# A hybrid RWKV-7 and DeltaNet layer on one core: a block inverse stepped on 32x32 tiles, and a third of the modulation sums moved behind the woven part

## Chip, cores and metric

One Trainium2 chip, one of its cores. The metric is the device time of one execution in microseconds (us); three timed runs of the kernel before gave 2334.98 to 2337.48, median 2336.01.

## What is computed

One layer over 256 latent tokens with 256 context tokens, width 2048, fp32. Cut to what matters here:

```python
mod = silu(c) @ w_ada + b_ada                 # 6 x 2048 columns
sh1, sc1, gt1, sh2, sc2, gt2 = split(mod, 6)
h = rmsnorm(x, norm1_w) * (1 + sc1) + sh1     # the same for the context: hc
# two token mixers on h @ w_in, hc @ w_in, in both directions of time
o_a = rwkv7(...)      # 16 heads of 64, chunked in the kernel: needs (I + L)^-1 of 64 x 64 blocks
o_b = gdn(...)        # 8 heads of 128, chunks of 64: needs (I + L)^-1 too
m = sigmoid(g_a) * (o_a @ p_a) + sigmoid(g_b) * (o_b @ p_b)
x = x + gt1 * (m @ w_out)
x = x + gt2 * swiglu(rmsnorm(x, norm2_w) * (1 + sc2) + sh2)
return rmsnorm(x, final_norm_w)
```

The second scale is `sc2`, columns 4 x 2048 to 5 x 2048 of `mod`. Of the six blocks of 1024 columns that the kernel calls `ada_rest`, blocks 0 and 1 are gt1, 2 and 3 are sh2, 4 and 5 are sc2.

## The kernel before, in words

**Products.** Weights come from HBM as fp32 chunks of up to 8 x 128 rows by 128 columns (`raw`, 512 KB). ScalarE rounds a chunk to fp32r (`hi`, L356), VectorE subtracts to get the rest (`lo`, L357), and `gemm` (L366 to L368) issues three products per 128 rows: hi by Xh, hi by Xl, lo by Xh. Three raw buffers and two each of hi and lo are in flight. Loads go out on SP's queue.

**Stages.** First the modulation of the first norm (to some 130 us). Then the *woven part*, to some 1388 us: generators for the input products (`products`, `cast`), the RWKV pairs (`prepare`, `grams`, `inverse`, `values`, `scan`, eight pairs of heads), the eight DeltaNet heads (`features`, `tokens`, `decays`, `head_grams`, `head_inverse`, `head_scan`) and `ada_rest`. Then merge A (`o_a @ p_a`, L1496), merge B (`o_b @ p_b`, L1514), the output product (L1528), which also casts four tiles of the first FFN weights, and the FFN with its 44 gate and up tiles and 16 down tiles.

**What sets the order.** In the woven part a planner (`Weave`, L169) runs the generators: each yields operations, the planner gives each a duration by formulas (`Lane`; a small matmul costs 0.024 us if its contraction is under 64 rows, L132), takes the operation that can start first, a lower rank winning ties, and emits it. PE, VectorE, ScalarE and POOL then run that order whatever the real times are. The RWKV pairs have ranks from 0, the heads from 100, the sums of `ada_rest` rank 500 and the products 900. Behind the woven part the framework orders instructions by its own timeline, except those kept in program order.

**The inverse** (`invert`, L552). Per call `nu` units of two 64x64 triangular blocks (16 for an RWKV pair, 8 for a DeltaNet head), half for each direction. The 16x16 blocks on the diagonal are inverted by VectorE (15 pairs of multiply and add, L583), after a round trip through DRAM that lays them out; T0 and its transpose Tx then hold them. The step from 16x16 to 32x32 (L613 to L624) runs once per direction: a group of 64x64 matmuls with 32 moving columns, a multiply with the mask `qmask`, a second group, an add into T0, and a transpose into Tx. The step from 32x32 to 64x64 (L641 on) works on 32x32 tiles of the array. `head_inverse(h)` waits for `inv`, h - 1, and builds the 128x128 inverse (TF) at its end; `head_scan(h)` needs it.

**The sums** (`ada_rest`, L1423). Per block and 128 rows of `w_ada`: one load of 128 x 1024 on POOL's queue, and two VectorE operations of 512 columns that multiply by silu(c) and add to `acc` (ScalarE for the first rows). After 16 of them four matmuls with ones sum over the partitions, VectorE copies the row out, two transposes turn it, and it is added to the bias into `mod`. In merge A POOL also multiplies each product with its gate (L1517), and ScalarE's sigmoids (L1500) wait for one load of 4 MB of gates.

Of the kernel before, what the change touches and what calls it, by code (L numbers as in the profile page):

```python
# [35 lines left out]
_C = {}  # L36
_n = 0
for _name, _w in (("ident", 128), ("ones", 128), ("bd64", 128), ("rmask", 256),
                  ("qmask", 64), ("tri", 256), ("aft", 256), ("q4", 4), ("q2", 2),
                  ("eps", 1), ("gneps", 1)):  # L40
    _C[_name] = (_n, _n + _w)
    _n += _w
# [12 lines left out]
def const_array():  # L55
    c = np.zeros((P, NC_COLS), np.float32)

    def put(name, a):
        lo, hi = _C[name]
        c[:, lo:hi] = np.asarray(a, np.float32).reshape(P, hi - lo)  # L60

    i = np.arange(P)
    put("ident", np.eye(P))
    put("ones", np.ones((P, P)))
    put("bd64", (i[:, None] // 64) == (i[None] // 64))
    s, t = (i % 64)[:, None], np.arange(64)[None]
    put("rmask", np.concatenate([t > s, t >= s, t < s, t <= s], 1))
    rb, cb = s // 16, t // 16
    same = (rb // 2) == (cb // 2)
    even = np.arange(64) // 16 % 2 == 0  # L70
    put("qmask", np.concatenate([(same & (rb % 2 == 1))[:, even], (same & (rb % 2 == 0))[:, ~even]], 1))
    u = i[:, None]
    v = i[None]
    put("tri", np.concatenate([u <= v, u >= v], 1))
    put("aft", np.concatenate([u > v, u < v], 1))
    put("q4", (i[:, None] % 4) == np.arange(4)[None])
    put("q2", (i[:, None] % 2) == np.arange(2)[None])
    put("eps", np.full((P, 1), 1e-6))
    put("gneps", np.full((P, 1), 64e-5))
    return c  # L80
# [30 lines left out]
class Lane:  # L111
# [5 lines left out]
    def __getattr__(self, name):  # L117

        def op(out, *a, **k):
# [6 lines left out]
            if name == "transpose" and len(a) == 2:  # L126
                cost = 0.109
            elif split:
                cost = 0.0065 + 0.000443 * n
            elif name == "matmul":  # L130
                rows, m = a[0].shape[0], out.shape[0]
                if rows < 64:  # L132
                    cost = 0.024
                elif rows == 64:
                    cost = max(0.066, 0.027 + 0.0008 * n)
                elif rows < P or m == P:
                    cost = 0.0054 + 0.00167 * n
                else:
                    cost = 0.107
            else:  # L140
                cost = self.fixed + self.each * n
# [126 lines left out]
def emit(ctx: ExitStack, tc, A, out, dbg=None):  # L268
# [31 lines left out]

    ident, ones, bd64 = c_("ident"), c_("ones"), c_("bd64")
    rmask = c_("rmask").rearrange("p (d k) -> p d k", d=2)
    qmask = c_("qmask").rearrange("p (d a c) -> p d a c", d=2, a=2)
    tri = c_("tri").rearrange("p (d t) -> p d t", d=2)
    aft = c_("aft").rearrange("p (d t) -> p d t", d=2)
    eps, gneps = c_("eps"), c_("gneps")
# [245 lines left out]
    def invert(pool, Lt, parts, nu, which, full, fill):  # L552
# [49 lines left out]
            return Tx[64 * h:64 * h + 64, u, :]  # L602


        def half(t, d):
            ax = "p u"[:2 * len(t.shape) - 3]
            return t.rearrange(f"{ax} (a b c) -> {ax} a b c", a=2, b=2)[..., d, :]

        def mm(ps, d, lhs, rhs):
            return [e.matmul(ps[64 * h:64 * h + 64, 32 * i:32 * i + 32], lhs(h, h2 * d + i), rhs(h, h2 * d + i),  # L610
                             start=True, stop=True) for i in range(h2) for h in range(2)]

        Qm = xt[:, :32 * nu].rearrange("p (u c) -> p u c", c=32)  # L613
        for d in range(2):
            T0d = half(T0[:, us[d]], d)
            ps = yield pib
            yield mm(ps, d, Lt, lambda h, u: half(N_(h, u), d))
            pv = ps[:, 0:32 * h2].rearrange("p (i a c) -> p i a c", a=2, c=16)
            yield v.tensor_mul(Qm[:, us[d]].rearrange("p i (a c) -> p i a c", a=2), pv,
                               qmask[:, d].unsqueeze(1).to_broadcast([P, h2, 2, 16]))  # L620
            yield mm(ps, d, Nt_, lambda h, u: Qm[64 * h:64 * h + 64, u, :])
            yield v.tensor_add(T0d, pv, T0d)
            weave.release(pib)
            yield v.transpose(Tx[:, us[d]], T0[:, us[d]])  # L624


        quads = []
# [795 lines left out]
    def ada_rest():  # L1423
# [20 lines left out]
                    yield s.activation(a, w[:, n:n + 512], AF.Identity, scale=ck[:, 0, 0:1])  # L1444
            weave.ready("added", i)

        for i in range(6 * KT):
            if i > 2:
                yield "added", i - 3
            weave.add(500, row_tile(i))  # L1450
# [33 lines left out]


    wstep[0] = 8
    gates_ctx = ExitStack()
    gp = gates_ctx.enter_context(tc.tile_pool(name="gp", bufs=1, reuse_waits="tile", side="right"))
    PA = gp.tile([P, KT, T], F32, name="PA")
# [6 lines left out]
    for j in range(KT):  # L1496
        ps = pst(pmm, "mm")
        gemm(ps[:, 0:T], load_w(A["pa"][j], P, 8), Oa, T)
        S.copy(PA[:, j], ps[:, 0:T])
        tc.keep_in_program_order(S.activation(gts[:, 2 * j:2 * j + 2, :], gts[:, 2 * j:2 * j + 2, :], AF.Sigmoid))  # L1500
    tc.keep_in_program_order(S.preload_act_table_set(LNEXP))

# [11 lines left out]
    for j in range(KT):  # L1514
# [4 lines left out]
        V.tensor_mul(m, ps[:, 0:T], gts[:, 16 + j])  # L1519
        V.tensor_add(m, m, PA[:, j])  # L1520
        split(M[0][:, j], M[1][:, j], m)

    gates_ctx.close()
    zap = ent(tc.tile_pool(name="zap", bufs=1, reuse_waits="tile", side="right"))
# [3 lines left out]
    for j in range(KT):  # L1528
# [3 lines left out]
        sq = square_sum(x1p, x1[:, j, :], ssum, j == 0)  # L1532
        if 0 < j < KT - 1:
            V.tensor_add(ssum, ssum, sq)
        if j % 3 == 2 and j < 12:
            w4.append(load_w(A["wgu"][j // 3], P, KT, into=[W4[:, i, j // 3] for i in range(2)] + [zap]))
    r = rms_scale(x1p, [ssum, sq], T, "rs")
    m_ctx.close()


    with tc.tile_pool(name="fp", bufs=1, reuse_waits="tile") as fp:
# [157 lines left out]
```

## Time and profile before

| what | value |
|---|---|
| median of three timed runs | 2336.01 us |
| the profiled execution, own time | 2348.77 us |
| its span from the first to the last instruction | 2346.7 us |
| busy share of the span: PE, VectorE, ScalarE, POOL | 95%, 66%, 45%, 5% |
| mean granted TensorE clock | 0.975 of full speed |

A row of the trace gives the engine (PE matmuls, DVE VectorE, ACT ScalarE, POOL, SP), the line of the code, the operation, out<-in by names and shapes. In the woven part every instruction has the line of the planner's helper, L142, so tiles tell them apart: `pi` is the inverse's accumulator, `mm` the products', `aw` the sums' tiles. A matmul busy time is not its cost in a stream; the distance between starts is.

### The profile page before, as it was taken

What the parts mean: (1) busy time and instruction counts of PE and PEld (TensorE: products, weight loads), DVE (VectorE), ACT (ScalarE), POOL (GpSimd) and SP (SyncE); (2) the same over time, 40 slices, a digit from 0 to 9 for tenths busy, and PEclk for the clock granted to TensorE, in tenths of its full rate; (3) what the DMA queues carried; (4) which work ended last, traced back from release to release, by engine and by line L of the source; (5) the groups of instructions that cost most, each with busy time, mean ns of one, the idle gap of its engine ahead of it and who ended that gap; (6) DMA issues with size and microseconds to landing.
All of it is one profiled execution on the core that took longest, in us unless ns stands there. A gap on an engine that the chain in (4) does not pass through costs nothing. (4 is left out here: it accounts for less than half of the span.)

```text
span 2346.7 us, 51488 instructions
## 1 busy us (share of the span) xinstructions
PE 2223.8 (95%) x21368; PEld 1951.7 (83%) x21368; DVE 1557.2 (66%) x3237; ACT 1047.9 (45%) x1863; POOL 113.5 (5%) x183
## 2 busy tenths in 40 slices
PE   7988999999999999999798999999999999999998
PEld 4767677778788777776677989999999999999997
DVE  3447588778986489889878645765666556545454
ACT  3246454544355544344234346544444444444443
POOL 0000000000000011111111003000000000000000
PEclk9999999999999999999789999999999999999999
DMA  9956454434344256657466565663777776566665
GB/s 377 397 148 189 152 134 102 111 83 117 100 109 133 85 172 207 189 167 217 145 191 194 182 219 180 209 214 107 239 233 234 234 238 218 187 185 194 191 191 165
DMA packets 232570, 430.58 MB, mean 183 GB/s; under 512 B 114832, under 2 KB 130064, under 8 KB 227984
## 3 DMA queue, kind: packets, MB, share of 16 engines
q1 hardware_dynamic: 204688, 351.78, 48.4%
q0 software_dynamic: 13824, 50.34, 7.0%
q10 hardware_dynamic: 13824, 25.17, 3.5%
q8 instruction: 167, 2.74, 0.5%
q14 instruction: 67, 0.55, 0.1%
HBM read 401.45 MB, written 25.77 MB: 182 GB/s over the span
## 5 line engine op out<-in xcount | busy, mean ns | idle before, releaser
L357 DVE TENSOR_TENSOR wlo<-wraw,whi 128x1024 fp32r<-128x1024 f32 x328 | 393.5, 1200 | 351.1 <-ACT whi L356 348.2
L356 ACT CAST whi<-wraw 128x1024 fp32r<-128x1024 f32 x328 | 337.7, 1030 | 472.8 <-PE mm L367 413.8
L142 PE MATMUL mm<-hxh,wlo 128*128 128x256 f32 (+1 forms) x1376 | 468.3, 340 | 9.9 <-DVE wlo L142 9.7
L142 PE MATMUL mm<-hxh,whi 128*128 128x256 f32 (+1 forms) x1376 | 469.0, 341 | 3.4 <-ACT whi L142 3.3
L142 PE MATMUL mm<-hxl,whi 128*128 128x256 f32 (+1 forms) x1376 | 468.3, 340 | 0.0
L368 PE MATMUL mm<-hfh,wlo 128*128 128x256 f32 x1344 | 377.1, 281 | 0.4 <-DVE wlo L357 0.4
L366 PE MATMUL mm<-hfh,whi 128*128 128x256 f32 x1344 | 376.5, 280 | 0.0
L367 PE MATMUL mm<-hfl,whi 128*128 128x256 f32 x1344 | 375.2, 279 | 0.0
L142 PEld LDWEIGHTS mm<-hxh,wlo 128*128 128x128 f32 x1376 | 265.6, 193 | 39.4 <-DVE wlo L142 13.0
L142 PEld LDWEIGHTS mm<-hxh,whi 128*128 128x128 f32 x1376 | 265.6, 193 | 31.5 <-issue 6.5
L142 PEld LDWEIGHTS mm<-hxl,whi 128*128 128x128 f32 x1376 | 265.8, 193 | 27.2 <-issue 6.1
L142 DVE TENSOR_TENSOR wlo<-wraw,whi 128x512 fp32r<-128x512 f32 x344 | 236.2, 690 | 62.7 <-ACT whi L142 60.0
L142 ACT CAST whi<-wraw 128x512 fp32r<-128x512 f32 x344 | 205.8, 618 | 112.1 <-PE mm L142 88.9
L366 PEld LDWEIGHTS mm<-hfh,whi 128*128 128x128 f32 x1344 | 253.4, 189 | 0.0
L368 PEld LDWEIGHTS mm<-hfh,wlo 128*128 128x128 f32 x1344 | 252.8, 188 | 0.6 <-DVE wlo L357 0.6
L367 PEld LDWEIGHTS mm<-hfl,whi 128*128 128x128 f32 x1344 | 253.2, 188 | 0.0
L142 DVE TENSOR_TENSOR arena<-arena 128x28 f32<-128x28 f32 (+13 forms) x538 | 132.0, 247 | 32.1 <-DMA arena<-scr 20.4
L366 PE MATMUL mm<-za,whi 128*128 128x256 f32 x512 | 141.8, 277 | 0.0
L367 PE MATMUL mm<-za,whi 128*128 128x256 f32 x512 | 141.7, 277 | 0.0
L368 PE MATMUL mm<-za,wlo 128*128 128x256 f32 x512 | 141.6, 277 | 0.0
L142 DVE SCALAR_TENSOR_TENSOR aw<-aw,ck 128x512 f32<-128x512 f32 x180 | 131.2, 739 | 5.1 <-DMA aw<-ada_rest 4.4
L368 PEld LDWEIGHTS mm<-za,wlo 128*128 128x128 f32 x512 | 96.2, 188 | 0.0
(311 smaller groups left out, 3924.5 us busy)
## 6 DMA issues: line engine op xcount, KB each, us to landing
wraw<-w SPq DMA_DIRECT2D x172, 512.0 KB, 4.3
wraw<-wgu SPq DMA_DIRECT2D x168, 512.0 KB, 4.5
aw<-ada_rest POOLq DMA_DIRECT2D x96, 512.0 KB, 4.7
aw<-ada_first SPq DMA_DIRECT2D x32, 1024.0 KB, 11.5
wraw<-wdn SPq DMA_DIRECT2D x64, 448.0 KB, 3.7
wraw<-wout SPq DMA_DIRECT2D x32, 512.0 KB, 4.7
aw<-ada_gt ACTq DMA_DIRECT2D x64, 256.0 KB, 5.0
wraw<-wdn SPq DMA_DIRECT2D x32, 512.0 KB, 3.6
```

The source lines that it names most:

```text
L142: return Op(self, cost, lambda: getattr(self.engine, name)(out, *a, **k), split)
L356: S.copy(hi[:, c, :M], raw[:, c, :M])
L357: V.tensor_sub(lo[:, c, :M], raw[:, c, :M], hi[:, c, :M].bitcast(F32))
L366: E.matmul(ps, hi, Xh[:, k, :n], start=first and i == 0, stop=False)
L367: E.matmul(ps, hi, Xl[:, k, :n], start=False, stop=False)
L368: E.matmul(ps, lo, Xh[:, k, :n], start=False, stop=last and i == len(wt) - 1)
```

## The change

It makes the 16-to-32 step of both directions at once on 32x32 tiles: one group of matmuls of 32 rows by 16 columns into `pv[:, 0]`, two multiply-adds with a row mask `low16` and an identity `eye16`, a second group into `pv[:, 1]`, copies of the new 16 columns into T0 (four by VectorE, four by ScalarE), and one transpose of all of T0. The planner's price of a small matmul changes with it. And `ada_rest` ends after four blocks; the generator `scale2` does blocks 4 and 5 with operations of 1024 columns, one tile per product of merge A, one per product from the 14th of merge B, and the rest in the output product.

```diff
@@ class Lane
                 if rows < 64:
-                    cost = 0.024
+                    cost = 0.009 if n <= 16 else 0.0125
@@ def invert
-        def half(t, d):
-            ax = "p u"[:2 * len(t.shape) - 3]
-            return t.rearrange(f"{ax} (a b c) -> {ax} a b c", a=2, b=2)[..., d, :]
-
-        def mm(ps, d, lhs, rhs):
-            return [e.matmul(ps[64 * h:64 * h + 64, 32 * i:32 * i + 32], lhs(h, h2 * d + i), rhs(h, h2 * d + i),
-                             start=True, stop=True) for i in range(h2) for h in range(2)]
-
-        Qm = xt[:, :32 * nu].rearrange("p (u c) -> p u c", c=32)
+        fours = [(h, u, 32 * b, slice(64 * h + 32 * b, 64 * h + 32 * b + 32)) for u in range(nu) for h in range(2) for b in range(2)]
+        Qm = xt[:, :16 * nu].rearrange("p (u c) -> p u c", c=16)
+        ps = yield pib
+        pv = ps[:, 0:32 * nu].rearrange("p (k u c) -> p k u c", k=2, c=16)
+        yield [e.matmul(pv[r, 0, u], Lt(h, u)[b:b + 32, b:b + 32], T0[r, u, b + 16 * (u // h2):b + 16 * (u // h2) + 16],
+                        start=True, stop=True) for h, u, b, r in fours]
         for d in range(2):
-            T0d = half(T0[:, us[d]], d)
-            ps = yield pib
-            yield mm(ps, d, Lt, lambda h, u: half(N_(h, u), d))
-            pv = ps[:, 0:32 * h2].rearrange("p (i a c) -> p i a c", a=2, c=16)
-            yield v.tensor_mul(Qm[:, us[d]].rearrange("p i (a c) -> p i a c", a=2), pv,
-                               qmask[:, d].unsqueeze(1).to_broadcast([P, h2, 2, 16]))
-            yield mm(ps, d, Nt_, lambda h, u: Qm[64 * h:64 * h + 64, u, :])
-            yield v.tensor_add(T0d, pv, T0d)
-            weave.release(pib)
-            yield v.transpose(Tx[:, us[d]], T0[:, us[d]])
+            yield v.scalar_tensor_tensor(Qm[:, us[d]], pv[:, 0, us[d]], low16[:, d:d + 1],
+                                         eye16[:, d].unsqueeze(1).to_broadcast([P, h2, 16]), ALU.mult, ALU.add)
+        yield [e.matmul(pv[r, 1, u], Tx[r, u, b:b + 32], Qm[r, u, :], start=True, stop=True) for h, u, b, r in fours]
+        for h in range(2):
+            yield [(s.copy if h else v.tensor_copy)(T0[r, us[d], b + 16 * d:b + 16 * d + 16], pv[r, 1, us[d]])
+                   for d in range(2) for b in (0, 32) for r in (slice(64 * h + b, 64 * h + b + 32),)]
+        weave.release(pib)
+        yield v.transpose(Tx, T0)
@@ def ada_rest
-        for i in range(6 * KT):
+        for i in range(4 * KT):
@@ behind the woven part
+    adp = ad_ctx.enter_context(tc.tile_pool(name="adp", bufs=1, reuse_waits="tile"))
+    def scale2():
+        for b in (4, 5):
+            acc = adp.tile([P, 1024], F32, tag="acc", name="acc")
+            for k in range(KT):
+                w = adp.tile([P, 1024], F32, tag="aw", name="aw", bufs=3)
+                G.dma_start(w, A["ada_rest"][b, :, k, :])
+                if k:
+                    tc.keep_in_program_order(V.scalar_tensor_tensor(acc, w, ck[:, k, 0:1], acc, ALU.mult, ALU.add))
+                else:
+                    tc.keep_in_program_order(V.tensor_scalar_mul(acc, w, ck[:, 0, 0:1]))
+                if k == KT - 1:
+                    ps = pst(pa, "pa")
+                    for j in range(4):
+                        E.matmul(ps[32 * j:32 * j + 32, 0:T], ones[:, 0:32], acc[:, T * j:T * j + T], start=True, stop=True)
+                    arow = adp.tile([P, T], F32, tag="arow", name="arow")
+                    V.tensor_copy(arow, ps[:, 0:T])
+                    for q in range(2):
+                        E.transpose(ps[:, T + P * q:T + P * q + P], arow[:, P * q:P * q + P], ident)
+                    for q in range(2):
+                        o = slice(32 + 8 * b + q, 40 + 8 * b, 2)
+                        V.tensor_add(mod[:, o], ps[:, T + P * q:T + P * q + P:32], p_("bada")[:, o])
+                yield
+    scale_next = scale2()
@@ merge A, after S.copy(PA[:, j], ...)
+        next(scale_next)
@@ merge B, after split(M[0][:, j], M[1][:, j], m)
+        if j > 12:
+            next(scale_next)
@@ output product, after the add into ssum
+        for _ in itertools.islice(scale_next, 1):
+            pass
```

The masks `low16` (2 columns) and `eye16` (32) take the place of `qmask` (64) among the constants.

## Rows read from the trace of the kernel before

**Rows 1.** Stretches: from:to, length, busy PE, PEld, DVE, ACT, POOL, clock, DMA.
```profile
240.00:840.00 600.00, 591.76 (x7267) 458.89 (x7266) 453.43 (x1116) 294.11 (x700) 18.97 (x45) 0.99 0.41 111
840.00:1178.40 338.40, 302.37 (x2416) 242.64 (x2414) 289.95 (x712) 140.05 (x254) 55.68 (x87) 0.93 0.63 188
1178.40:1314.90 136.50, 123.08 (x1140) 107.80 (x1138) 109.25 (x279) 54.41 (x109) 14.76 (x23) 0.95 0.65 199
1314.90:1384.80 69.90, 68.59 (x721) 65.72 (x721) 41.80 (x114) 29.63 (x61) 0.00 (x0) 1.00 0.55 162
1388.50:1445.00 56.50, 52.00 (x404) 50.82 (x405) 25.42 (x33) 35.69 (x67) 19.57 (x15) 0.91 0.65 215
1445.00:1491.00 46.00, 44.20 (x368) 43.41 (x367) 37.02 (x62) 23.76 (x33) 1.66 (x1) 0.96 0.60 195
1491.00:1593.00 102.00, 93.62 (x775) 90.85 (x773) 62.63 (x76) 50.25 (x61) 0.00 (x0) 1.00 0.65 214
```

**Rows 2.** Timeline, ScalarE and VectorE, two head borders: start, length, operation.
```profile
1035.03 0.76 ACT L142 COPY TF<-pi 64x256 f32<-64x256 f32 x2 [3.92 <-PE pi L142]
1036.44 0.42 DVE L142 STREAM_TRANSPOSE T<-LT 64x256 f32<-64x256 f32 x1
...
1100.19 0.76 ACT L142 COPY TF<-pi 64x256 f32<-64x256 f32 x2 [1.03 <-PE pi L142]
1102.65 0.42 DVE L142 STREAM_TRANSPOSE T<-LT 64x256 f32<-64x256 f32 x1
```

**Rows 3.** Timeline, PE, around one group of the step in an RWKV pair.
```profile
350.38 0.40 PE L142 MATMUL mm<-hxl,whi 128*128 128x512 f32 x1
350.62 0.39 PE L142 MATMUL mm<-hxh,wlo 128*128 128x512 f32 x1
350.94 1.12 PE L142 MATMUL pi<-arena 64*64 64x32 f32 x32
351.89 0.96 PE L142 MATMUL pa<-LAl,arena 64*64 64x128 f32 x26
```

**Rows 4.** Timeline, PE, around a group on 32x32 tiles, last head.
```profile
1352.36 0.45 PE L142 MATMUL pi<-T,LT 32*32 32x32 f32 x32
1352.74 0.39 PE L142 MATMUL mm<-hxh,wlo 128*128 128x256 f32 x1
1352.96 0.28 PE L142 MATMUL mm<-hxh,whi 128*128 128x256 f32 x1
1353.08 0.28 PE L142 MATMUL mm<-hxl,whi 128*128 128x256 f32 x1
```

**Rows 5.** Timeline, VectorE and ScalarE, copies on 32 partitions in the last head.
```profile
1354.63 0.59 DVE L142 COPY Tx<-pi 32x128 f32<-32x128 f32 x2 [0.85 <-PE pi L142]
1355.31 0.54 ACT L142 COPY Tx<-pi 32x128 f32<-32x128 f32 x2 [0.60 <-DVE Tx L142]
```

**Rows 6.** Timeline, VectorE, first and last operation of the second head's step.
```profile
945.26 0.28 DVE L142 TENSOR_TENSOR arena<-pi,C 128x128 f32<-128x128 f32 x1
...
954.75 0.43 DVE L142 STREAM_TRANSPOSE Tx<-T 128x256 f32<-128x256 f32 x1
```

**Rows 7.** VectorE's sums: whole run, then 1130 to 1314.9: count, busy us, mean ns.
```profile
L142 DVE SCALAR_TENSOR_TENSOR aw<-aw,ck 128x512 f32<-128x512 f32 x180 | 131.2, 739 | 5.1 <-DMA aw<-ada_rest 4.4 <-ACT aw L142 0.5
...
L142 DVE SCALAR_TENSOR_TENSOR aw<-aw,ck 128x512 f32<-128x512 f32 x62 | 44.6, 732 | 0.6 <-ACT aw L142 0.5
```

**Rows 8.** VectorE's subtraction of 1024 elements: two in merge A, then the whole run.
```profile
1424.50 1.23 DVE L357 TENSOR_TENSOR wlo<-wraw,whi 128x1024 fp32r<-128x1024 f32 x1 [1.49 <-ACT whi L356]
1427.22 1.23 DVE L357 TENSOR_TENSOR wlo<-wraw,whi 128x1024 fp32r<-128x1024 f32 x1 [1.49 <-ACT whi L356]
...
L357 DVE TENSOR_TENSOR wlo<-wraw,whi 128x1024 fp32r<-128x1024 f32 x328 | 393.5, 1200 | 351.1 <-ACT whi L356 348.2
```

**Rows 9.** Transfers: GB/s in 40 slices (whole run; 1388:1593), gates' load, POOL's wait.
```profile
GB/s 377 397 148 189 152 134 102 111 83 117 100 109 133 85 172 207 189 167 217 145 191 194 182 219 180 209 214 107 239 233 234 234 238 218 187 185 194 191 191 165
...
GB/s 234 352 362 204 98 118 193 206 206 199 191 146 291 141 180 189 205 206 192 194 180 241 225 190 202 279 233 225 197 248 157 219 230 238 279 149 219 160 193 225
...
gts<-gts__1351 SPq DMA_DIRECT2D x1, 4096.0 KB, 14.2
...
POOL PA L1517 <- ACT gts L1500: 112.4, 1, 112.4
```

**Rows 10.** Waits between 1388 and 1593 us: total us, times, longest us.
```profile
ACT w L356 <- DMA wr<-wgu: 16.7, 8, 3.3
...
PE mm L368 <- DVE wlo L357: 6.0, 8, 1.3
```

More of the change, by code (lines that the diff above doesn't have):

```diff
@@ L38 @@
 for _name, _w in (("ident", 128), ("ones", 128), ("bd64", 128), ("rmask", 256),
-                  ("qmask", 64), ("tri", 256), ("aft", 256), ("q4", 4), ("q2", 2),
+                  ("low16", 2), ("eye16", 32), ("tri", 256), ("aft", 256), ("q4", 4), ("q2", 2),
                   ("eps", 1), ("gneps", 1)):
@@ L67, in const_array @@
     put("rmask", np.concatenate([t > s, t >= s, t < s, t <= s], 1))
[L68 to L71, printed above, removed]
+    below = (i // 16 % 2 == 1)[:, None]
+    put("low16", np.concatenate([below, ~below], 1))
+    same = (i % 16)[:, None] == np.arange(16)[None]
+    put("eye16", np.concatenate([same & ~below, same & below], 1))
     u = i[:, None]
@@ L302, in emit @@
     rmask = c_("rmask").rearrange("p (d k) -> p d k", d=2)
-    qmask = c_("qmask").rearrange("p (d a c) -> p d a c", d=2, a=2)
+    low16 = c_("low16")
+    eye16 = c_("eye16").rearrange("p (d c) -> p d c", d=2)
     tri = c_("tri").rearrange("p (d t) -> p d t", d=2)
@@ L1486, in emit @@
     wstep[0] = 8
+    ad_ctx = ExitStack()
+    adp = ad_ctx.enter_context(tc.tile_pool(name="adp", bufs=1, reuse_waits="tile"))
[22 more added lines that the diff above has]
+    scale_next = scale2()
     gates_ctx = ExitStack()
@@ L1538, in emit @@
     m_ctx.close()
+    ad_ctx.close()
     with tc.tile_pool(name="fp", bufs=1, reuse_waits="tile") as fp:
```

## The prediction

> **What bounds the kernel now.** The first view is the table of stretches [rows 1]; its last columns tell which limit holds where. From 240 to 840 us, while the RWKV pairs are woven, PE is busy 591.8 of 600 us at a granted clock of 0.99: any TensorE time taken out there shortens the run. From 840 to 1178.4 and on to 1314.9 us, the eight DeltaNet heads, PE has 36 and 13.4 us free at 0.93 and 0.95, while VectorE is busy 86% and 80%. The limit there is neither, but a chain, as the timeline at a head's border shows [rows 2]: ScalarE writes the last block of one head's inverse (ends 1035.79) and the next head's inverse starts at 1036.44. The next border, at 1100.95 and 1102.65, is the same; of the seven only the first is looser. So a head lasts as long as its inversion, 66 us between these two starts. The tail from 1314.9 to 1384.8 is TensorE again (68.6 of 69.9). The merge and output products are 52.0 of 56.5, 44.2 of 46 and 93.6 of 102 us on PE, so they are TensorE's too, with VectorE at 25, 37 and 63 us.
>
> **The step, on TensorE.** A matmul here is two instructions in the trace. An RWKV inversion has 16 units, and its 16-to-32 step makes four groups of 16 matmuls on 64x64 tiles, 32 instructions each. One starts at 350.94 and the next instruction at 351.89 [rows 3]: 0.95 us, 30 ns per instruction. The new step makes two groups of 64 matmuls on 32x32 tiles with 16 columns. The nearest row is the next step's group on 32x32 tiles with 32 columns [rows 4]: 32 instructions between 1352.36 and 1352.74, 11.9 ns each. I take that row, though half the columns may cost less: 256 x 11.9 ns = 3.05 us against 4 x 0.95 = 3.80, a gain of 0.75. Two groups fewer also spare two changes between the fp32r products and the small ones: 0.32 us before the group where the products start 0.24 apart [rows 3], and 0.22 instead of 0.12 behind it [rows 4], so about 0.2 each, 0.4 together. Eight inversions: 8 x 1.15 = **-9 us**. The ends: at half of 11.9 ns for half the columns 8 x 2.7 = -21; at the 30 ns of the 64x64 row 256 x 30 = 7.7 us, 8 x (7.7 - 3.8 - 0.4) = +28. The Trainium skill ("TensorE: Matmul & The Clock Gate", section "Wait — 56ns, not 53.3ns?") speaks against the change: matmuls, it says, never start less than about 25 ns apart, however few columns they have. By it this term would be an estimated 8 x (256 x 25 ns - 3.8 - 0.4) = +18 in place of -9. The trace disagrees, with 11.9 ns from start to start [rows 4].
>
> VectorE's share stays: two multiplies, two adds and two transposes go; two multiply-adds, four copies on 32 partitions and one double transpose come. ScalarE gets four new copies, 0.27 us each by the row of such copies [rows 5]; it is busy 294 of 600 us [rows 1], so that costs nothing in itself. Nor do the smaller constants. The planner is now told 9 or 12.5 ns for a 32x32 matmul where two instructions take 23.8 [rows 4]: it will expect an RWKV group 64 x 14.8 ns = 0.9 us too early and queue VectorE's multiply-adds so. With VectorE busy 453 of 600 us and PE the limit, that wait is covered; in the heads, at half the size, it is part of the hand-overs below.
>
> **The step, in the chain of the heads.** In the second head it runs from 945.26 to 955.18 [rows 6], 9.9 us. Its operations are short: two multiplies and two adds of 0.28, two transposes of 0.43, and three groups of 16 instructions at 30 ns, in sum 3.4 us. The other 6.5 us are six hand-overs between TensorE and VectorE, 1.1 us each, in which the chain stands behind other work. The new chain has four: multiply-adds to TensorE, TensorE to VectorE's copies, those to ScalarE's copies, and these to the transpose. (ScalarE's copies of the next step wait for VectorE's, with a wait of 0.60 us put down to them [rows 5], and I expect that order again.) 4 x 1.1 + 0.5 + 0.8 + 1.1 + 1.0 + 0.7 = 8.5 us, a gain of 1.4 per head; for the first five heads **-7 us**, between 0 (ScalarE's new place eats it) and 5 x 4 = -20. In the last head the products bind, and it gains TensorE's time alone, 4 x 0.48 - 1.52 + 0.4 = 0.8: **-1 us**.
>
> **The sums that leave the weave.** All six blocks make 180 VectorE operations of 739 ns and 131.2 us [rows 7]. Blocks 4 and 5 are a third; the last 62, 44.6 us, run between 1130 and 1314.9. They have the lowest rank, yet each one that starts holds a chain operation back by up to 0.7 us. What can be won is capped by PE's free 13.4 us in heads 5 and 6 [rows 1]. I take 12 there with the step's own gain, and 2 in head 4: **-14 us**, between 0 and -25 (PE's 13.4, the step, and clock). The sums' loads on POOL's queue go with them, and nothing waits there.
>
> The weave gains 9 + 7 + 1 + 14 = 31 us.
>
> **The sums in the merge.** Each of 32 tiles brings one load of 512 KB on POOL's queue and one operation on 1024 elements. Bounds for it: 1.20 us, the subtraction of that size, and 2 x 0.739 = 1.48 [rows 7, 8]; I take 1.25, nearest the single long operation. 32 x 1.25 = 40 us of VectorE work lie beside 203 us of products; what counts is where VectorE can give 1.25 us without a cast being late.
> - Merge A, 16 tiles. A product lasts 2.72 us and VectorE idles 1.49 of it [rows 8]: a tile fits with 0.24 to spare if it has landed. The transfers compete: in this stretch they move 215 GB/s, in its first 15 us 352 and 362, where the best of the whole run is 397 [rows 9]. There the 4 MB of gates land (14.2 us), and ScalarE's sigmoids and then POOL's 16 multiplies wait for them [rows 9]; a load issued behind such a multiply in POOL's queue comes late, and VectorE's sum, with the cast subtractions queued behind it, waits. Price: 3 us for gates landing later, 3 for late tiles, **+6** (0 to +16).
> - Merge B, 3 tiles. VectorE is busy 37 of 46 us, 2.3 of 2.9 per product, so some 0.6 is free: 3 x (1.25 - 0.6) = 2, and 1.5 more for the output product's first weights, which stand behind; **+3.5** (1 to 6).
> - Output product, 13 tiles. VectorE has 39 us free of 102, but in the four of 16 products that also cast early FFN weights it has none: ScalarE waits 16.7 us for eight such loads, and over the three loops PE 6.0 us for late subtractions [rows 10]. Four tiles cost their 1.25, and eight loads come about 0.4 later: **+8** (2 to 20).
> - TensorE sums up the two blocks here, about 1 us each with changes: **+2**. In the weave this lay under the chain and gave nothing back. The late block is done by the 13th output product, before anything reads it.
>
> In sum +19.5.
>
> **The number.** -31 + 19.5 = about -12, against the profiled execution's 2348.8 us, which stands 12.8 above the median of the runs, 2336.0. I carry the difference over: 2324.
>
> **Rivals.**
> 1. The sums find room: the weave gains its 31, and the merge costs the 2 us on TensorE and 2 more. For it: 1.49 us idle in each product of merge A. Against: the transfers. 2336 - 27 = 2309. Chance 0.17.
> 2. The heads do not follow: without the sums, VectorE stands idle where it worked and the chain is as long as before, so the heads win 4 us and not 21; -9 - 1 - 4 + 19.5 = +5, 2341; with merge A cheaper by 5, 2336. For it: the hand-overs [rows 6] stand behind other operations than the sums too. Chance 0.14.
> 3. Slower: a sum whose tile has not landed stands in VectorE's queue ahead of the next weights' subtraction. Place: all three loops. It decides once the loads reach what the transfers can move; in merge A 1 MB per 2.72 us is 385 GB/s, and 397 is the best seen [rows 9]. Then no tile is hidden: 32 x 1.25 = 40, and 8 for gates and early weights, 2 on TensorE: +50 - 31 = +19, 2355. Chance 0.17.
> 4. The small matmuls start no closer than the 64x64 ones, 30 ns [rows 3]: +28 in the RWKV pairs where I have -9, and in a head 128 x 30 ns = 3.8 us against 1.9, which eats the chain's gain of 7 and turns the tail to +1.5: 28 + 1.5 - 14 + 19.5 = +35, 2371. Against it stand the rows with 11.9 ns. Chance 0.04. By the Trainium skill's 25 ns of that same section this rival would end some 10 us lower, an estimate by the term above.
>
> **How the numbers follow.** My forecast has 0.48, its own range 2313 to 2331. 0.2% is 4.7 us, about what a measurement can tell from no change. Faster: 0.48 + 0.17 + 0.02 of rival 2 = 0.67; same: 0.10 of rival 2; slower: 0.02 of it + 0.17 + 0.04 = 0.23. The range runs from 2300, below rival 1 by part of the weave's bounds, to 2346, where part of rival 3 is left out.
>
> **What would show it.** In the profile after: inversion groups of 128 instructions on 32x32 tiles lasting 1.3 to 1.6 us (at 3 us rival 4 holds); RWKV stretch shorter by 9; head borders still within 1 us of each other, heads 5 and 6 shorter by 5 or more (unchanged: rival 2); 32 operations of about 1.25 us in the merge; merge A to output 220 to 225 us instead of 204.5, with PE waiting for late subtractions (over 240: rival 3). I am wrong if the planned order of the woven part changes by more than these sums, or if the transfers decide merge A.

## The result and the profile after

The changed kernel takes 2344.39 us (median of 19 runs, 2337.86 to 2355.76), the kernel before on the same chips 2339.88 (19 runs, 2334.3 to 2346.32). The ratio is 1.0027 with a 95% interval of 1.0014 to 1.0039: some 6 us slower by it. The prediction was 12 us faster. Its range (2300 to 2346) holds the time; the direction is wrong.

Where the time went, by the borders that the prediction used (first head's start, last product of the woven part, first product of merge A, last loop before the FFN). The view is the table of stretches, first of the changed kernel, then of the kernel before at its own borders; the columns are those of [rows 1]:

```profile
240.00:853.10 613.10, 586.08 (x8287) 452.03 (x8286) 456.18 (x1119) 300.27 (x728) 16.86 (x45) 0.98 0.40 108
853.10:1367.30 514.20, 470.66 (x4765) 400.88 (x4763) 404.94 (x1048) 227.04 (x454) 52.65 (x82) 0.96 0.54 167
1379.10:1436.60 57.50, 52.21 (x403) 50.24 (x404) 41.24 (x43) 34.10 (x62) 22.32 (x30) 0.94 0.92 326
1436.60:1484.00 47.40, 46.75 (x392) 45.79 (x391) 40.60 (x71) 25.86 (x36) 0.93 (x2) 1.00 0.62 218
1484.00:1609.40 125.40, 110.70 (x879) 107.40 (x878) 92.48 (x124) 55.92 (x77) 6.36 (x12) 0.96 0.68 232
```

```profile
240.00:839.20 599.20, 590.97 (x7264) 458.24 (x7263) 452.63 (x1115) 293.69 (x699) 18.97 (x45) 0.99 0.41 112
839.20:1384.60 545.40, 494.65 (x4277) 416.79 (x4275) 441.79 (x1103) 224.51 (x424) 70.44 (x110) 0.94 0.62 187
1388.60:1445.50 56.90, 52.48 (x409) 51.31 (x409) 25.88 (x33) 36.08 (x67) 20.06 (x16) 0.92 0.65 214
1445.50:1492.70 47.20, 45.41 (x378) 44.61 (x377) 37.91 (x65) 24.75 (x35) 1.16 (x1) 0.96 0.60 195
1492.70:1607.20 114.50, 105.34 (x851) 102.57 (x850) 73.96 (x103) 56.08 (x76) 0.00 (x0) 0.97 0.60 198
```

| us | before | after | difference | predicted |
|---|---|---|---|---|
| start to the first head (RWKV pairs) | 839.2 | 853.1 | +13.9 | -9 |
| heads and tail | 545.4 | 514.2 | -31.2 | -22 |
| wait ahead of merge A, and merge A | 60.9 | 69.3 | +8.4 | +6 |
| merge B | 47.2 | 47.4 | +0.2 | +3.5 |
| output product to the FFN | 114.5 | 125.4 | +10.9 | +10 |
| FFN and down product | 739.5 | 740.1 | +0.6 | 0 |

The sum is +2.8 between the two profiled executions, which stand 7 (after) and 9 us (before) above their kernels' medians of 19. Behind the woven part +19.5 was predicted and +19.5 is there. The miss is in the RWKV pairs, by 23 us; the heads and tail come out 9 us better than predicted. The view of TensorE's waits from 240 to 853.7 us says what is new in them; columns: total us, times, longest:

```profile
PE pi L142 <- issue: 7.4, 9, 2.3
PE s L142 <- issue: 4.8, 2, 3.4
PE s L142 <- ACT R L142: 3.5, 2, 2.7
PE mm L142 <- ACT whi L142: 3.0, 1, 3.0
```

In the kernel before, the same view of 240 to 840 us has of these only

```profile
PE pi L142 <- issue: 0.5, 1, 0.5
```

"Issue" is time in which the engine waited for nothing that the profile shows: 12.8 us in 12 places (the twelfth, 0.6 us, at a `pa` group), all inside or shortly behind the small groups of an inversion. TensorE's timeline around the first, and two stretches of the table around it:

```profile
260.50 0.28 PE L142 MATMUL mm<-hxh,whi 128*128 128x256 f32 x1
260.71 1.16 PE L142 MATMUL pi<-arena,Tx 32*32 32x16 f32 x117
264.13 0.39 PE L142 MATMUL pi<-arena,Tx 32*32 32x16 f32 x11 [2.26 <-issue]
264.45 0.58 PE L142 MATMUL mm<-hxl,whi 128*128 128x256 f32 x1
264.83 0.41 PE L142 MATMUL mm<-hxh,wlo 128*128 128x256 f32 x1
265.05 0.41 PE L142 MATMUL mm<-hxh,whi 128*128 128x256 f32 x1
```

```profile
240.00:263.50 23.50, 20.11 (x301) 10.94 (x300) 4.19 (x9) 11.25 (x16) 0.00 (x0) 1.00 0.74 219
263.60:270.20 6.60, 6.07 (x38) 6.03 (x38) 4.63 (x9) 2.88 (x7) 0.00 (x0) 0.50 0.28 82
```

The group stops 11 rows short of its 128, and the trace names nothing that it waits for. From 263.6, near the end of the stop, to 270.2 TensorE is granted 0.50 of its clock (1.2 GHz of 2.4), so the products that follow start 0.22 us apart (264.83, 265.05) and not 0.12 [rows 4]. What it lacked can be read on the page: the queue that carries instructions (before, then after; packets, MB, share):

```profile
q8 instruction: 167, 2.74, 0.5%
```

```profile
q8 instruction: 179, 2.93, 0.5%
```

TensorE has 22904 matmul rows and as many weight loads after (21368 before), in sum 3072 instructions more, and the queue 12 packets more: 256 instructions to a packet. A packet holds 16 KB (2.93 MB over 179), so an instruction has 64 bytes, and a packet is 128 matmul rows with their weight loads. One group of the new step is just such a packet. The packets' times bear it out. In the stop shown, one of them is on its way from 261.82 to 262.87 and TensorE goes on at 264.13; the view of transfers from 261.5 to 264.5 us has this one packet:

```profile
q8 instruction: 1, 0.02, 2.2%
```

So it is with all twelve stops: the last packet ahead of each stop's end lands 1.26 to 1.50 us before TensorE goes on. Where nothing stops a group, it runs in 1.19 us, by TensorE's timeline of another inversion:

```profile
351.27 1.26 PE L142 MATMUL pi<-arena 32*32 32x16 f32 x128
352.46 0.50 PE L142 MATMUL mm<-hxl,whi 128*128 128x512 f32 x1
```

### The profile page after: what moved, and what is told of

Read it like the earlier page. It is cut to its first block, busy times and chain, and to the rows that moved or that the text cites. A ratio compares the mean times of both kernels' runs of the same rounds, so it can differ in the third digit from the quotient of the medians.

```text
span 2349.5 us, 54635 instructions
## 1 busy us (share of the span) xinstructions
PE 2204.3 (94%) x22904; PEld 1936.3 (82%) x22904; DVE 1563.2 (67%) x3225; ACT 1058.2 (45%) x1922; POOL 103.0 (4%) x183
## 3 DMA queue, kind: packets, MB, share of 16 engines
q1 hardware_dynamic: 204688, 351.77, 47.2%
q8 instruction: 179, 2.93, 0.5%
## 4 chain that ended last, share of the span: by engine, by line
PE 73%; DVE 10%; DMA 8%; ACT 4%; issue 3%; SPq 1%; POOL 0%; DVEq 0%; ACTq 0%; POOLq 0%
PE mm L142 21%; PE mm L369 12%; PE mm L367 12%; PE mm L368 12%; PE s L142 6%; PE pa L142 5%; DVE arena L142 4%; PE pi L142 2%; DVE wlo L142 2%; DMA aw<-ada_rest 1%; DMA wr<-wgu 1%; DVE aw L142 1%; PE mm L455 1%; ACT arena L142 1%; DMA tscr<-arena 1%
## 5 line engine op out<-in xcount | busy, mean ns | idle before, releaser
L142 DVE TENSOR_TENSOR arena<-arena 128x28 f32<-128x28 f32 (+12 forms) x538 | 131.8, 247 | 17.2 <-DMA arena<-scr 7.6
L368 PEld LDWEIGHTS mm<-za,whi 128*128 128x128 f32 x512 | 96.3, 188 | 0.0
L367 PEld LDWEIGHTS mm<-za,whi 128*128 128x128 f32 x512 | 96.3, 188 | 0.0
```

The source lines that it names most:

```text
L142: return Op(self, cost, lambda: getattr(self.engine, name)(out, *a, **k), split)
L367: E.matmul(ps, hi, Xh[:, k, :n], start=first and i == 0, stop=False)
L368: E.matmul(ps, hi, Xl[:, k, :n], start=False, stop=False)
```

## The experiments

All ratios are to the kernel before on the same chip, with 95% intervals.

**1. The parts alone.** *The step alone*, with its new price: `ada_rest` back to six blocks, `scale2` and its calls out.

```diff
-        for i in range(4 * KT):
+        for i in range(6 * KT):
```

> The step alone, all six blocks of sums back in the woven part. Theory A: in the changed kernel TensorE stands still for 12.8 us in 12 places beside the small groups of the RWKV inversions, where the trace names no releaser (one place and 0.5 us in the kernel before); I take this for instructions that have not arrived, since the new step has 512 of them per inversion more than before counts for the same work. Then the step alone keeps these waits (10 to 15 us), the first head starts about 14 us late (853 instead of 839), the heads win 7 to 15 of it back, and the whole is 0 to 8 us above the kernel before. Theory B (the sums' move reorders the pairs, the step is innocent): first head at 830 to 840, 9 us faster than before.

Measured: 2342.63, ratio 1.0018 (1.0002 to 1.0033). First head at 851.97; 12.1 us of waits without releaser ahead of it. Theory B falls: the step, with its price, moves the first head by itself.

*The sums' move alone*: the step, its constants and its price as before; of the diff stand `ada_rest`'s four blocks, `scale2` and its calls.

```diff
-                    cost = 0.009 if n <= 16 else 0.0125
+                    cost = 0.024
...
-        fours = [(h, u, 32 * b, slice(64 * h + 32 * b, 64 * h + 32 * b + 32)) for u in range(nu) for h in range(2) for b in range(2)]
+        def half(t, d):
```

> The move of the sums alone, with the old step and the old planner costs. Theory A: no waits without a releaser above 1 us in sum before the first head, which starts at 839 as before; the heads win 15 to 25 us; the gap ahead of the merge grows by some 4 to 8 us as in the changed kernel (11.8 us against 3.8), the output product by 11. In sum 2 to 8 us faster than before. Theory B: the first head is 14 us late here too, and the whole 5 to 10 us slower than before.

Measured: 2318.72, ratio 0.9922 (0.9908 to 0.9936): 18 us faster, more than twice what I expected and the opposite of the prediction, whose terms for the move sum to +5.5. No wait without a releaser above 0.4 us, first head at 837.2. Wait ahead of the merge to FFN: 234.5 us against 222.6, +12 and not +19.5. (The step alone, whose code behind the woven part is that of before, shows 216.3 there: single profiles of this stretch differ by 6 us.) Heads and tail: 510.1 against 545.4, -35 and not -14. The heads that the sums leave, by the table of stretches, before and with the sums moved; the last row of before is a piece at half clock within its first head, which sets in during a pause of TensorE of 3.3 us:

```profile
1102.65:1178.40 75.75, 60.06 (x441) 46.40 (x440) 58.53 (x148) 29.36 (x49) 11.60 (x20) 0.81 0.55 163
1178.40:1251.40 73.00, 67.44 (x557) 56.20 (x556) 62.10 (x150) 29.71 (x56) 10.40 (x17) 0.94 0.63 191
1251.40:1314.90 63.50, 55.65 (x584) 51.60 (x583) 47.14 (x130) 24.70 (x54) 4.36 (x7) 0.95 0.66 208
...
1145.50:1155.70 10.20, 9.36 (x53) 7.82 (x54) 8.76 (x17) 2.10 (x4) 1.65 (x3) 0.50 0.43 126
```

```profile
1099.30:1164.00 64.70, 55.57 (x451) 42.84 (x450) 49.37 (x134) 27.73 (x48) 5.20 (x7) 0.95 0.37 116
1164.00:1217.80 53.80, 53.80 (x503) 46.51 (x503) 40.43 (x116) 21.50 (x46) 1.28 (x1) 1.00 0.32 94
1217.80:1270.10 52.30, 49.33 (x536) 45.28 (x536) 35.23 (x107) 27.48 (x55) 4.14 (x5) 1.00 0.54 173
```

212.3 us become 170.8 (the tail takes 7.5 back, with products that moved there). Of the 41.5, 17.0 are PE's idle time and 24.5 its busy time: 92 matmul rows fewer, which are among those that moved to the tail, and the rest at clocks of 0.95 to 1.00 where they had 0.81 to 0.95. I had capped the gain by the idle time.

*The new step in the heads alone*, and *the old price* in the changed kernel:

```diff
+        if nu == 16:
+            def half(t, d):
...
+        else:
             fours = [(h, u, 32 * b, slice(64 * h + 32 * b, 64 * h + 32 * b + 32)) for u in range(nu) for h in range(2) for b in range(2)]
```

```diff
-                    cost = 0.009 if n <= 16 else 0.0125
+                    cost = 0.024
```

> The changed kernel with the old step on 64x64 tiles in the RWKV inversions (16 units) and the new one in the heads (8 units), planner costs as changed. Theory A: the waits without a releaser go (under 1 us), the first head starts at 836 to 842, all that the heads won stays, and the kernel is 8 to 14 us faster than the changed one, some 5 to 9 faster than before. Theory C (the planner's lower prices for small matmuls make the order of the RWKV pairs worse): the first head is still 8 to 14 us late though no small group of the new kind is left there, since the next step's 32x32 groups carry the new price too.

> The changed kernel with the planner's old price of 24 ns for a matmul on 32x32 (9 and 12.5 in the change, 23.8 measured in the trace before). Theory A: the waits without a releaser stay at 8 to 15 us and the time within 4 us of the changed kernel. Theory C: the first head starts at 836 to 842 and the kernel is 8 us or more faster than the changed one.

Measured: heads_step 2324.04, ratio 0.9956 (0.9940 to 0.9973), waits without releaser 1.9 us, first head at 845.1. Theory A is right on the waits, all but 1.9 us, and on the way the time goes: 17 us faster than the changed kernel by the ratios, where 8 to 14 were expected; the first head is 845 and not 836 to 842, so theory C has a share. old_price 2340.07, ratio 1.0008 (0.9991 to 1.0025), waits 9.9 us, first head at 844.5. Against the 837.2 of the sums alone the price delays the first head by 8 us, the step by 7, and both by 16. That is no exact account: in the seven kernels here with the old step and the old price in the pairs, the one before among them, the first head starts between 833.0 and 839.2.

**2. Rate or count; the price by itself; the groups by themselves.** *spread*: the old price, and in the RWKV pairs each group in two halves,

```diff
+        for f in ([fours] if nu < 16 else [fours[:32], fours[32:]]):
+            if f is not fours and f[0] is not fours[0]:
+                yield 1.0
```

> The changed kernel with the planner's old price, and each of the two groups of the step in an RWKV inversion cut in two halves of 32 matmuls with a pause of 1 us in the plan between them, which the planner fills with products; the count of instructions is that of the changed kernel. Theory A (instructions that have not arrived, a matter of rate): the waits without a releaser fall from 9.9 us to under 4 and the time falls by 8 us or more against the kernel with the old price alone (2340). Rival (the count of instructions or their places matter, not the rate): waits and time unchanged within 4 us, or up by the two more changes between products and small matmuls, 8 x 0.8 = 6 us.

Measured: 2329.05, ratio 0.9950 (0.9933 to 0.9968), first head at 841.0, waits without releaser 3.1 us, by TensorE's waits up to there:

```profile
PE pi L142 <- issue: 3.1, 4, 1.4
```

With as many instructions, spread out, the ratio falls from 1.0008 to 0.9950, 14 us. It is not their count. (That the halves lie at other places among the products goes with the edit; *small_groups* below has the rate alone.)

*heads_step with the old price:*

> The new step in the heads alone, as in the run named heads_step, but with the planner's old price of 24 ns. Theory C (the lower price moves the RWKV pairs back): the first head starts at 836 to 840 instead of 845, the waits without a releaser stay below 2 us, and the time is 4 to 8 us below that run's 2324. If the step is worth anything in the heads, it is below 2317; if it ends at 2317 to 2321, the step gives the heads nothing once the sums are gone.

Measured: 2322.84, ratio 0.9925 (0.9904 to 0.9945), no wait without releaser, first head at 833.9. The start of the first head by the view of the tile LT, first and last start in each row (heads_step, this kernel, then old_price):

```profile
L146 DVE STREAM_TRANSPOSE T<-LT x16: 425/436/443, 845.1 to 1264.9; 64x256 f32<-64x256 f32 x16
L146 DVE STREAM_TRANSPOSE T<-LT x16: 423/436/443, 833.9 to 1254.8; 64x256 f32<-64x256 f32 x16
L142 DVE STREAM_TRANSPOSE T<-LT x16: 425/436/444, 844.5 to 1264.7; 64x256 f32<-64x256 f32 x16
```

The price is worth 11 us of the first head's start (6 to 12 by the spread named above) and 7 us by the ratios (0.9956 to 0.9925; different chips). With it gone the step in the heads ends where the kernel without the step ends (0.9922), though its five first heads take 314.0 us (833.9 to 1147.9) against 326.8.

*small_groups*: groups of small matmuls in a kernel that does nothing else.

```diff
+        for i in range(n):
+            a = size * (i % (P // size))
+            r = slice(a, a + size)
+            c = i // (P // size) % (512 // cols)
+            E.matmul(ps[r, cols * c:cols * c + cols], big[r, 3072:3072 + size], big[r, 3200:3200 + cols], start=True, stop=True)
```

> No part of the reference is computed: eleven groups of small matmuls alone, each behind some 6 us of VectorE work, with 128, 128, 128, 256, 512 (16 columns), 512 (32 columns) on 32x32 tiles, 256 on 64x64 with 32 columns, then 128 and 128 beside four loads of 512 KB, 512 beside sixteen, and 128. Theory A: at 11.9 ns from start to start a group of 128 (256 in the trace) takes 3 us without a stop or stops once; from some length on, TensorE stops again and again with no releaser named, so that 512 take well over 12.2 us (20 or more), and longer still beside the loads; on 64x64 tiles at 30 ns there is no stop. Rival (the waits in the changed kernel come from something else): all groups run at 11.9 to 13 ns per instruction, 512 in 12.2 to 13.3 us.

Measured, TensorE's timeline in the group of 512 matmuls (1024 rows) alone, then in the one beside sixteen loads of 512 KB:

```profile
77.23 1.90 PE L299 MATMUL ps<-big 32*32 32x16 f32 x128 [2.10 <-issue]
80.95 1.90 PE L299 MATMUL ps<-big 32*32 32x16 f32 x128 [1.83 <-issue]
84.41 1.91 PE L299 MATMUL ps<-big 32*32 32x16 f32 x128 [1.55 <-issue]
88.14 1.91 PE L299 MATMUL ps<-big 32*32 32x16 f32 x128 [1.82 <-issue]
...
217.21 1.90 PE L299 MATMUL ps<-big 32*32 32x16 f32 x128 [4.57 <-issue]
223.41 1.90 PE L299 MATMUL ps<-big 32*32 32x16 f32 x128 [4.29 <-issue]
229.60 1.90 PE L299 MATMUL ps<-big 32*32 32x16 f32 x128 [4.29 <-issue]
```

128 rows in 1.9 us, a stop, 128 rows, a stop: the packet of the instruction queue to the row. (The 1.9 us, where the changed kernel has 1.19, are those of half clock, as told at the end.) From start to start 3.46 to 3.73 us, 27 to 29 ns per row in the mean, and 6.2 us beside loads. The 512 matmuls take 29.6 us (73.65 to 103.21) where 11.9 ns would give 12.2. After 6 us of rest or more the first stop came behind 91 to 223 rows. The 64x64 group has no stop. The packets of the instruction queue go with it: between 78 and 100 us they start 3.3 to 3.7 us apart, and TensorE goes on 1.2 to 1.6 us behind the landing of each. Theory A is shown with nothing else in the kernel.

*sums_places*: the sums alone, with eight tiles in merge B and eight in output products without early FFN weights.

```diff
-        if j > 12:
+        if j % 2:
             next(scale_next)
...
-        for _ in itertools.islice(scale_next, 1):
-            pass
         if j % 3 == 2 and j < 12:
...
+        else:
+            for _ in itertools.islice(scale_next, 1):
+                pass
```

> The kernel with the sums moved alone (2318.7), with eight tiles in the second merge products (every other one) and eight in the output products, none of them in the four that also cast early FFN weights. My account of the output product (the four crowded products cost their tiles, +11 us against before): the stretch of the output product falls by 4 to 6 us, the second merge stretch grows by 2 to 4, in sum 0 to 4 us faster. Rival (what the output product lost are transfers and TensorE's block sums): no change within 2 us.

Measured: 2320.19, ratio 0.9918 (0.9900 to 0.9936). From table load to table load of ScalarE the output stretch is 116.2 us (122.4 with the sums alone), merge B 51.2 (48.8), merge A 61.2 (59.8 from its first product): the account of the output product is right in this one trace, and the whole is the same as without.

**3. The wait ahead of the merge.** TensorE's waits there, before and after:

```profile
PE mm L366 <- ACT oah L371: 3.8, 1, 3.8
PE mm L367 <- ACT oah L372: 11.8, 1, 11.8
```

In six of six profiles the load of the RWKV heads' output starts 0.31 us behind the start of the last gate product, whose operand lies where that load writes. Before, 3.6 us of the last head's outputs came behind its start and hid part of a load of 6.9 us; after, nothing did, and the load took 11.3 beside the sums' first tiles. *oad_early* loads it elsewhere:

```diff
-    Q.dma_start(PA[:, 0:8], oad.rearrange("k p t -> p k t"))
+    O8 = adp.tile([P, 8, T], F32, name="O8")
+    Q.dma_start(O8, oad.rearrange("k p t -> p k t"))
```

> The changed kernel with one difference: the RWKV heads' output (8 KB a partition) is loaded into memory of the pool with the sums' tiles instead of memory that the last gate product still reads. In six of six profiles that load starts 0.31 us after the start of the last gate product, and in the changed kernel TensorE waits 11.8 us for it (3.8 before). My account: the product's memory holds the load back; with it gone the wait falls to under 3 us and the time by 7 to 10 us (2335 to 2338). Rival (the woven part's last outputs or the crowded transfers hold the merge back): the wait stays above 7 us and the time within 3 us.

Measured: 2348.01, ratio 1.0029 (1.0017 to 1.0042). The wait is gone and the time is not. TensorE's first merge product of this kernel (timeline), then its merge A (table of stretches):

```profile
1366.91 0.39 PE L367 MATMUL mm<-oah,whi 128*128 128x256 f32 x1 [0.49 <-ACT oah L372]
```

```profile
1366.90:1434.30 67.40, 51.38 (x403) 49.49 (x404) 45.63 (x45) 35.41 (x64) 21.02 (x32) 0.87 0.89 310
```

Merge A starts 12 us earlier and lasts 67.4 us instead of 57.5: with the wait 67.9 against 69.3. Its transfers, the gates' 4 MB, the 8 MB of products' weights and 8 MB of sums' tiles, run at 326 GB/s in the changed kernel (214 before), with DMA engines busy 0.92. The wait ahead of it was time in which they ran. So my account of the wait was right and its price wrong.

**4. Versions beyond the change.** *combined*: step in the heads, old price, other places, early load; *combined_old_step*: the same with the old step.

> The new step in the heads alone, the old price, the sums' tiles in other places (16, 8 and 8, beside no early FFN weights) and the early load of the RWKV heads' output. From the runs of the parts: 2323 for step in the heads with the old price, 8 to 10 off for the wait ahead of the merge (11.5 us there), 0 to 2 for the places: 2311 to 2315. If it comes out at 2318 or above, what the woven part wins is given back behind it.

> The same with the old step everywhere: sums moved, other places, early load. The wait ahead of the merge was 3.6 us with the sums moved alone, so 1 to 3 us are won there and 0 to 2 by the places: 2314 to 2318. If the new step is worth its chain's 13 us in the heads (470 against 483 us from the first head's start to the last inverse's end), this ends 4 to 8 us above the run with the step in the heads; if the products set the end of the woven part, within 2 us of it.

Measured: 2319.11, ratio 0.9905 (0.9890 to 0.9919), and 2318.81, 0.9916 (0.9896 to 0.9936). Both are some 20 us faster than the kernel before and do not differ; the first misses its 2311 to 2315 by 4 us, and what it names for that case (given back behind) is what the profiles show. There the first merge product starts 9.5 us earlier with the step (1340.7 against 1350.2) and the stretch to the FFN is 5 us longer (231.8 against 226.6): by these two profiles half of what the heads win is given back in the merge and output products. That the transfers do it is argued from merge A above, not shown.

*half_moved*: the old step, only the last block moved, no tile in merge A.

```diff
-        for i in range(4 * KT):
+        for i in range(5 * KT):
...
-        for b in (4, 5):
+        for b in (5,):
```

> The old step and the old price, and only the last block of sums moved: 16 tiles, eight in the second merge products and eight in the output products, none in the first merge products, where the changed kernel and the one with the sums moved alone transfer 326 to 333 GB/s against 214 before. My account: the first merge products are bound by transfers once the tiles are there (with the wait ahead of them 67.9 to 69.3 us in the changed kernel and the one with the early load, 60.7 before), so they return to 59 to 62 us with their wait; the weave keeps half of what the sums' move won, 15 to 25 of 38 us; the second merge and output products cost 5 to 8 us. In sum 2318 to 2328. If it is below 2316, half the move is better than the whole; above 2330, the last block in the woven part costs more than its half.

Measured: 2345.43, ratio 1.0023 (1.0007 to 1.0040): a miss by 17 us and more. Its profiled execution is its fastest (2338.41). There the stretch to the FFN is 231.2 us with the wait, +8.6, and heads and tail 530.9, 14.5 less than before where I expected 15 to 25 less; the fifth head (1096.2 to 1169.6) still has a clock of 0.88. That half the move wins nothing, where the whole has 0.9922, is measured; why is open, as is why its other executions are up to 17 us slower than the profiled one.

## Why the prediction was wrong, step by step

The runs make a ladder, by their ratios to the kernel before on their own chips (in us of 2340):

| kernel | ratio | against before |
|---|---|---|
| sums moved alone | 0.9922 | -18 |
| and the step in the heads | 0.9925 | -18 |
| and the step in the pairs | 1.0008 | +2 |
| and the new price (the change) | 1.0027 | +6 |

**The step, on TensorE: the step that failed.** -9 was forecast; in the changed kernel's profile the pairs are 14 us longer. By the ladder the step in the pairs costs 19 us and the price 4 more. (Of the 19 the profiles show 8: 11 in the first head's start and 9 in heads and tail, less 11 behind them. The profiled execution with the old price is the fastest of twelve, 9 us below their median.)

"256 x 11.9 ns" scaled a group of 32 rows [rows 4] up to groups of 128. The matmul's own price was better than forecast: 1.19 us for a group that runs through, 9.3 ns from start to start, so 8 x (3.80 - 2.38) = 11 us won where the working has 6. But the group's 256 instructions are as many as one packet brings, and run in less time than the next takes to come (3.5 us in the kernel of small groups). The working has no term for the supply of instructions. That gave 12.8 us of stops, and half clock behind three of them: 27.3 us of the stretch are at half clock, against 10.2 before, 17.1 of them behind stops for instructions and 10.2 behind two waits for ScalarE. In sum, as an estimate from these: -11.4 for the rows and -3.2 for the spared changes (as forecast), +12.8 for stops, +8.5 of clock (half of 27.3 less 10.2), +6.5 for the two waits, +2.1 for nine product rows that now come ahead of the first head, which makes +15 where +13.9 is measured.

My range for this term (-21 to +28) held it, by the 64x64 row's 30 ns; rival 4 with that rate (chance 0.04) had nearly the right number, 27 to 29 ns over a long group, for a cause it did not name. Inside a packet it is wrong. The prediction's sentence on the Trainium skill fares likewise: the Trainium skill ("TensorE: Matmul & The Clock Gate", section "Wait — 56ns, not 53.3ns?") says that starts come no closer than about 25 ns, and rows here start 9.3 ns apart; its estimate of +18 comes near only because of the stops.

**The planner's price, "covered".** It was not: 845.1 against 833.9 us for the first head's start, with the step in the heads alone. The groups that are priced too low include the next step's on 32x32 tiles. How the wrong times turn into the later start is open. The two waits for ScalarE above (3.5 and 3.0 us) stand in all three profiles with the new step in the pairs and the new price, and are 0.9 us or less with the old price; but heads_step, with the new price and the old step there, has 0.8 us of the first and none of the second, and starts 11 us late all the same.

**The step, in the chain of the heads: right, and worth nothing.** In the second head it runs from 964.15 to 971.17 us:

```profile
964.15 0.28 DVE L142 SCALAR_TENSOR_TENSOR arena<-pi,C 128x64 f32<-128x64 f32 x1
...
967.72 0.90 DVE L142 COPY T<-pi 32x64 f32<-32x64 f32 x4 [0.92 <-PE pi L142]
970.47 0.70 DVE L142 STREAM_TRANSPOSE Tx<-T 128x512 f32<-128x512 f32 x1
```

That is 7.0 us where the old one [rows 6] took 9.9 and 8.5 was forecast. The five first heads gain 12.8 with it (7 forecast, 0 to 20). But the whole ends where it does without: 0.9925 against 0.9922. In the profiles of these two, heads and tail are 9 us shorter with the step and the wait ahead of merge A 8 us longer (11.5 against 3.6).

**The sums that leave the weave: mis-sized by 21 us.** -14 forecast, -35 measured in the profile of the move alone. The cap was "PE's free 13.4 us"; busy time shrank too, as the clock rose from 0.94 to 0.98 over heads and tail (545 x 0.06 = 33 us of clock lost before, 510 x 0.02 = 10 after). That the clock is this much of the 35 is an estimate from these two profiles.

**The sums in the merge: right in sum, in part by luck.** +19.5 in the changed kernel, +12 with the sums alone: 8 of the 19.5 are the longer wait ahead of merge A, which the working does not have and the sums alone do not bring (3.6 us). The 30 multiply-adds take 1.35 us each (1.25 forecast). Merge A pays by transfers, as written, but ahead of its first product: itself it lasts 57.5 us where it had 56.9; the output product pays in the four crowded products, as the other places showed. Merge B was free.

**The rivals.** 1 (sums find room) falls for the merge, which did cost 12 to 19.5. 2 falls: the heads did follow. 3 falls: from the first product of merge A to the first of the FFN, the forecast's borders, there are 216.9 us (205.2 before; 220 to 225 forecast, over 240 by rival 3), and VectorE waits 1.8 us in all for tiles. 4 is told above. Two terms were far off with opposite signs: in the profiles the pairs by +23 in the changed kernel, and the sums by -21 with the move alone (heads and tail in the changed kernel by -9). That the range holds the time is luck: it does so because the two offset each other, the one below its bound of -25, the other within the -21 to +28 of its term for a reason that the term does not have.

## What to carry to other kernels

Count instructions as a transfer: a group of small matmuls that uses up one packet of instructions faster than the next comes stops the engine, whatever one matmul costs; spread such groups between long products, or use larger tiles (512 rows on 64x64 tiles ran without a stop, if at half clock). Price a wait or its removal with the granted clock behind it, not by idle time alone. And undo the parts of a change one by one: here one part was worth 18 us and the other cost 24.

## What the runs showed of the hardware

- **Instructions can run out.** In the kernel of small groups, 128 matmul rows in 1.9 us with 128 weight loads, then 1.55 to 1.83 us of nothing, again and again; up to 4.57 us beside loads. In the changed kernel and three of its variants (the step alone, old_price, spread) all 37 such stops in the pairs end 1.24 to 1.53 us behind the landing of a packet of instructions. The Trainium skill ("Runtime: NRT & Kernel Launch", section "Instruction fetch mechanics") says that instructions come in blocks of 16 KiB, 256 of them, fetched while the former are worked off, and that this stays mostly hidden. The blocks agree to the row; that they stay hidden does not hold for these groups.
- **The price of a stop is more than the stop.** Behind a stop of 0.8 us (to 707.7) and within one of 3.4 us (to 713.4) the clock falls: 0.50 from 710.6 to 717.4.

```profile
700.00:710.40 10.40, 9.11 (x324) 7.81 (x323) 9.56 (x26) 2.21 (x6) 0.00 (x0) 1.00 0.36 103
710.60:717.40 6.80, 4.05 (x21) 3.93 (x21) 3.05 (x5) 2.16 (x7) 1.10 (x3) 0.50 0.07 24
717.60:775.00 57.40, 54.56 (x871) 43.19 (x870) 38.70 (x111) 31.11 (x83) 1.09 (x1) 1.00 0.41 107
```

- **Executions of one kernel differ by their clock.** The kernel with half the sums moved took 2338.4 us at a mean of 0.981 and 2355.3 at 0.972; with the sums moved alone, six executions lie between 2314.7 (0.985) and 2321.6 (0.981).
- **FFN and down product, which no run edits, took 737.9 to 748.2 us** in the profiles, at a granted clock of 1.00 and 0.99. No verdict on a kernel's time rests on a difference of single profiles below some 10 us; where a stretch is told by one, it is that profile's.
- **The kernel of small groups ran at half clock.** A row on 32x32 tiles with 16 columns takes 14.8 ns there and one on 64x64 54 ns (512 in 27.5 us), against 9.3 in the changed kernel and 30 in the kernel before [rows 3]. From start to start within a group they are 13.3 and 53 ns apart. In the other kernels rows of the two shapes start 8.5 and 29 ns apart at a granted clock of 1.00 and 13.4 and 52 at 0.50. Its profile gives 1.00, but its trace has no record of the clock at all. The stops are the same finding at either level: the changed kernel has them at 1.00.
